# Off-diagonal products of the delta net's triangular inverse, queued behind one more projection tile

## The chip, the cores and the metric

The kernel runs on one core of a Trainium2 chip. The metric is the device time of one execution in microseconds (us). The core has a matrix engine (TensorE, PE in the profile, with its weight loads as PEld), a vector engine (VectorE, DVE), a scalar engine (ScalarE, ACT), a general engine (GpSimd, POOL), and SyncE (SP), which here issues nearly all DMAs. Each engine works through one queue of instructions in order. A matmul writes into PSUM, and another engine has to read the result out ("evict" it) before that buffer can be written again.

## The reference

Two layers of a diffusion trunk run on 1152 tokens (1024 latent and 128 context tokens) of width 1024. Each layer is a token mixer and an MLP, each between modulated norms:

```
x = x + gate1 * norm(mixer(modulate(norm(x))))
x = x + gate2 * norm(w2 . relu(w1 . modulate(norm(x)))^2)
```

The mixer has one input projection that feeds four groups of heads: latent attention, windowed attention, a gated delta net that runs over the tokens in both directions, and a Hyena long convolution. Their outputs go through one output projection. The delta net is computed in chunks of 64 tokens:

```
a   = tril(kb . k^T * gam, -1)                    # 64 x 64 per chunk and head
sol = triangular_solve(a + I, [v*b, kb*exp(decay)])
u_v, w = sol[..., :dv], sol[..., dv:]
def step(S, xs):                                   # one chunk after the other
    u = uv_c - w_c . S
    o = qd_c . S + aqk_c . u
    return S * tl_c + kt_c^T . u, o
```

The triangular solve is what the change touches: the kernel builds the inverse of (a + I), transposed, for every chunk, head and direction, and multiplies with it.

## The kernel before

All large products are taken in three reduced-precision products (high x high, high x low, low x high), so a tile of projections is 3 chunks of tokens (384 columns each) x 8 slices of the width x 3 products = 72 matmuls. `proj_tile` (L499) makes one such tile of 128 output columns: each chunk gets a PSUM buffer `pj` from a pool of four (`self.P`, pool "P", L313), and its `sink` evicts it. For the Hyena tiles the sink (L518, L519) is two reads of `pj` by ACT. The token-major transposes of a Hyena tile (`ht`, three of them, evicted by ACT at L1748) take their buffers from the same four.

In each layer three Python generators are advanced by turns (`run_timed`), each by a clock of its own: `rest` makes the projections and then Hyena and attention, `other` prepares the delta net and scans it, and `adas` makes the modulation vectors of later stages (`ada`, with its weights `wada` by DMA). Whatever `other` emits is given a higher priority, and the scheduler of the framework then settles the order of each engine's queue by these priorities and by its own reckoning of times. The Hyena stage (`X`, `iz`) and the attention (`S`, `ST`, `O`) follow the projections in `rest`.

The tiles of a layer come in a fixed order: delta net inputs (5 tiles), its gate (2), six Hyena tiles (8th to 13th), the windowed values (14th), the latent keys (15th), two tiles of queries (16th, 17th), and four rotary tiles (18th to 21st).

`gdn_prep` runs once for each pair of heads, p = 0 and then p = 1. Around the change it does this:

- 31 steps of forward substitution on diagonal blocks of 32 (`N`, L1205 to L1214); direction 0 on DVE, direction 1 on POOL.
- ACT writes a transposed copy `Tb` of each `N` (L1217), SP writes `N` and `Tb` to DRAM (`nscr`, L1218, L1219) and reads them back in another layout: `NT` (L1229) and `NaT`, which lies in the tile `NaTG` (L1232).
- The off-diagonal blocks `G` are two small products one after the other: st = 0 is AT x NaT (32 x 32 each, 72 for two heads' worth of chunks), evicted by DVE (L1251), and st = 1 multiplies with NT and is evicted by ACT (L1257).
- Then `kd`, `wt` and `uv` follow with NT, and after p = 1 the scan `gdn_scan`: 18 serial steps, each with products `u` and `dS` on PE that wait for one another through DVE and ACT. Its outputs go to DRAM (`goscr<-sc`), from where the normed output is read (`o`).

The keys of the latent attention (`mla_keys`: `ct`, `kpT`, `k`, `v`) are also made in the stretch in which p = 1 is prepared.

Of the kernel before, what the change touches and what calls it, by code (L numbers as in the profile page):

```python
# [29 lines left out]
AT = 2  # L30
# [133 lines left out]
class Trunk:  # L164
# [334 lines left out]
    def proj_tile(self, l, j, hi, lo, sink, w=None):  # L499
        w = w or self.load_cols(self.I["wa"][l, j], "wa")  # L500
        for a, n in NCH:
            ps = self.P(name="pj")
            for k in range(8):
                self.mm3(ps[:, :n], w(k), [hi[k][:, a:a + n], lo[k][:, a:a + n]], k == 0, k == 7)
            sink(ps[:, :n], slice(a, a + n))

    def proj_raw(self, l, j, hi, lo, name):
        o = self.W(name=name)
        self.proj_tile(l, j, hi, lo, lambda ps, s: self.nc.scalar.copy(out=o[:, s], in_=ps))
        return o  # L510
# [579 lines left out]
    def gdn_prep(self, l, p, g, be, tag):  # L1090
# [76 lines left out]
        AQ, AT = [], []  # L1167
# [53 lines left out]
        NaT, G = X[:, 0], X[:, 1].rearrange("p m h c -> p h m c")  # L1221
# [12 lines left out]
            NTm.append(NT)  # L1234
        yield

        for st in range(2):
            for h in range(2):
                pg = self.P((9, 32), "G", "Q")
                for m in range(9):  # L1240
                    for dr in range(2):
                        ab, bb = dr * 32, 32 - dr * 32
                        for a in range(2):
                            ra = slice(a * 64 + ab, a * 64 + ab + 32)
                            rb = slice(a * 64 + bb, a * 64 + bb + 32)
                            if st == 0:
                                self.mm(pg[rb, m], AT[dr][ra, m, h, bb:bb + 32], NaT[ra, m, h])
                            else:
                                self.mm(pg[ra, m], G[rb, h, m], NTm[dr][rb, m, h, bb:bb + 32])
                if st == 0:  # L1250
                    V.tensor_copy(out=G[:, h], in_=pg[:, :9])  # L1251
                else:
                    for dr in range(2):
                        for a in range(2):
                            ra = slice(a * 64 + dr * 32, a * 64 + dr * 32 + 32)
                            bb = 32 - dr * 32
                            nc.scalar.activation(out=NTm[dr][ra, :, h, bb:bb + 32], in_=pg[ra, :9], func=AF.Copy, scale=-1.0)  # L1257
            yield
# [765 lines left out]
    def sink(self, l):  # L2024
        def f(kt, ps, s):
            w = s.stop - s.start
            t = self.H(name="osk")
            self.nc.scalar.copy(out=t[:, :w], in_=ps)
            self.nc.sync.dma_start(out=self.oscr[l, kt, :, s], in_=t[:, :w])
        return f  # L2030
# [5 lines left out]
    def layer(self, l):  # L2036
# [54 lines left out]
        if l == 0:  # L2091
            with self.tc.issue_after(self.lead.ins):
                self.late_consts()
        self.done = set()

        def until(x):
            while x not in self.done:
                yield 1
# [142 lines left out]
```

## Time and profile before

| | |
|---|---|
| median of 3 runs | 3825.18 us (3819.07 to 3829.11) |
| profiled execution, its own time | 3828.84 us |
| its span, first to last instruction | 3827.1 us |
| mean granted clock of TensorE | 0.938 of full speed |
| PE busy | 3531.1 us (92%) |
| DVE, ACT, POOL busy | 2279.6, 1355.6, 853.1 us |

The stages of a layer follow one another. In layer 0 the projections with the preparation of the delta net lie between about 150 and 490 us, the scan with Hyena between 490 and 680 us, the attention after that up to about 1010 us, and the MLP up to about 1900 us, in which PE is never idle. In layer 1 the same stages lie at about 2000 to 2375, 2375 to 2606, 2606 to 3000 and 3050 to 3811 us.

In a row of the timeline stand start, duration, engine, line, operation, output and inputs, partitions x elements, how many instructions were merged, and in brackets the idle time of the engine before it with what ended it.

### The profile page before, as it was taken

The numbers are of one execution on the slowest core, as the hardware profiler recorded it, in microseconds if no ns is written. First come the engines' busy times: TensorE is split into PE (matmuls) and PEld (weight loads), VectorE is DVE, ScalarE is ACT, GpSimd is POOL, SyncE is SP. The second block draws the span as 40 slices with busy tenths as digits, with TensorE's granted clock in tenths as the row PEclk, the third lists the DMA queues.
The fourth block names the chain that finished last, engine by engine and source line by source line (L and its number), as shares of the span: only waits on it lengthen the run. The fifth ranks groups of instructions, "written<-read, shape, count | busy, mean of one in ns | idle before, by whom it ended". The sixth has DMA issues, their size and how long they took to land. (4 is left out here: it accounts for less than half of the span.)

```text
span 3827.1 us, 57478 instructions
## 1 busy us (share of the span) xinstructions
PE 3531.1 (92%) x21710; PEld 2958.8 (77%) x21710; DVE 2279.6 (60%) x4583; ACT 1355.6 (35%) x2970; POOL 853.1 (22%) x806
## 2 busy tenths in 40 slices
PE   7989888899899999999989798787999999999998
PEld 4879764366689999999968797645666899999997
DVE  5765577696645444444586664768884544444446
ACT  5434343264542222122354234323564422222112
POOL 1151521264430000000131524213553200000003
PEclk9999889897899999999999898897889999999999
DMA  5356486831421111111234465756314211111113
GB/s 202 115 120 158 139 275 202 235 90 39 138 87 47 45 44 34 44 45 45 96 103 131 108 144 161 258 187 177 84 50 138 72 45 45 45 45 42 40 41 121
DMA packets 364672, 405.31 MB, mean 106 GB/s; under 512 B 115815, under 2 KB 237157, under 8 KB 364394
## 3 DMA queue, kind: packets, MB, share of 16 engines
q1 hardware_dynamic: 364394, 401.63, 34.9%
q8 instruction: 171, 2.80, 0.3%
q14 instruction: 107, 0.88, 0.1%
HBM read 298.34 MB, written 103.19 MB: 105 GB/s over the span
## 5 line engine op out<-in xcount | busy, mean ns | idle before, releaser
L213 PE MATMUL hid<-hT,w1h 128*128 128x384 f32 x3072 | 786.5, 335 | 0.1
L213 PE MATMUL pj<-hT,wah 128*128 128x384 f32 x2112 | 575.1, 351 | 9.0 <-ACT wah L253 4.2
L1831 DVE TENSOR_TENSOR acc<-acc,mo 128x512 f32<-128x512 f32 x504 | 346.1, 687 | 391.8 <-PE mo L213 391.8
L213 PEld LDWEIGHTS hid<-hT,w1h 128*128 128x128 f32 x3072 | 557.7, 188 | 14.4 <-ACT h L481 1.1
L213 PE MATMUL hid<-hT,w1l 128*128 128x384 f32 x1536 | 514.1, 335 | 0.0
L213 PE MATMUL mo<-w2h,ul 128*128 128x512 f32 x1116 | 435.0, 392 | 0.0
L213 PE MATMUL mo<-w2h,uh 128*128 128x512 f32 x1080 | 422.7, 391 | 0.0
L213 PE MATMUL mo<-w2l,uh 128*128 128x512 f32 x1080 | 422.7, 391 | 0.0
L213 PEld LDWEIGHTS pj<-hT,wah 128*128 128x128 f32 x2112 | 395.3, 196 | 21.9 <-issue 7.8
L662 POOL TENSOR_TENSOR e<-e,e 128x512 f32<-128x512 f32 (+1 forms) x216 | 307.3, 1424 | 313.8 <-DVE el L232 145.2
L269 POOL TENSOR_TENSOR postr<-postr,mhalf 128x1 f32<-128x1 f32 x36 | 22.3, 621 | 1568.9 <-DVE postr L268 1568.6
L213 PE MATMUL pj<-hT,wal 128*128 128x384 f32 x1056 | 367.5, 348 | 0.7 <-DVE wal L232 0.7
L242 ACT CAST w2h<-w 128x512 fp32r<-128x512 f32 x128 | 70.3, 619 | 732.9 <-PE mo L213 728.8
L213 PEld LDWEIGHTS hid<-hT,w1l 128*128 128x128 f32 x1536 | 288.3, 188 | 2.5
L232 DVE TENSOR_TENSOR el<-e,eh 128x512 fp32r<-128x512 f32 (+1 forms) x252 | 241.4, 977 | 25.1 <-ACT eh L653 20.4
L213 PEld LDWEIGHTS mo<-w2h,ul 128*128 128x128 f32 x1116 | 209.6, 188 | 46.1
L213 PEld LDWEIGHTS mo<-w2h,uh 128*128 128x128 f32 x1080 | 202.8, 188 | 37.5
L213 PEld LDWEIGHTS mo<-w2l,uh 128*128 128x128 f32 x1080 | 202.7, 188 | 36.5
L213 PEld LDWEIGHTS pj<-hT,wal 128*128 128x128 f32 x1056 | 206.3, 195 | 4.6 <-issue 2.0
L1814 DVE SCALAR_TENSOR_TENSOR relu<-hid,relu 128x384 f32<-128x384 f32 x180 | 99.5, 554 | 166.9 <-ACT relu L1813 166.9
L213 PE MATMUL ada<-wada,cst 128*32 128x512 f32 x384 | 130.8, 692 | 45.5 <-DMA wada<-in_w_ada 45.4
L232 DVE TENSOR_TENSOR wal<-wa,wah 128x512 fp32r<-128x512 f32 x88 | 67.6, 773 | 147.2 <-ACT wah L253 118.2
(502 smaller groups left out, 6366.6 us busy)
## 6 DMA issues: line engine op xcount, KB each, us to landing
w<-in_w SPq DMA_DIRECT2D x256, 256.0 KB
wada<-in_w_ada SPq DMA_DIRECT2D x192, 256.0 KB
wa<-in_wa SPq DMA_DIRECT2D x88, 256.0 KB
x<-xres SPq DMA_DIRECT2D x21, 512.0 KB
x<-in_x SPq DMA_DIRECT2D x18, 512.0 KB
Q<-rscr SPq DMA_DIRECT2D x32, 288.0 KB
o<-oscr SPq DMA_DIRECT2D x18, 512.0 KB
xres<-x SPq DMA_DIRECT2D x36, 256.0 KB
```

The source lines that it names most:

```text
L213: self.last = self.nc.tensor.matmul(out, l, r, start=start, stop=stop, skip_group_check=True)
L232: self.nc.vector.tensor_tensor(out=lo, in0=x, in1=hi.bitcast(F32), op=ALU.subtract)
L242: self.nc.scalar.copy(out=hi[:, q], in_=st)
L269: self.nc.gpsimd.tensor_tensor(out=out, in0=out, in1=self.bcs(self.mhalf[:out.shape[0]], out.shape), op=ALU.pow)
L662: self.nc.gpsimd.tensor_tensor(out=acc, in0=acc, in1=e, op=ALU.add)
L1814: nc.vector.scalar_tensor_tensor(out=r[:, :n], in0=ps[:, :n], scalar=0.0, in1=r[:, :n], op0=ALU.max, op1=ALU.mult)
L1831: nc.vector.tensor_tensor(out=acc[t][:, ns], in0=acc[t][:, ns], in1=ps, op=ALU.add)
```

## The change

Each tile of projections now leaves its last matmul in a list (`tiles`, emptied for each layer). In `gdn_prep`, ahead of the off-diagonal products, the generator waits until 11 (p = 0) or 18 (p = 1) tiles have been emitted, handing the turn to the other generators meanwhile. The products of st = 0 then get an order edge: on PE they stand behind the last matmul of the newest tile. Nothing is computed differently, and no instruction is added.

```diff
@@ proj_tile
             sink(ps[:, :n], slice(a, a + n))
+        self.tiles.append(self.last)
@@ gdn_prep
+        while len(self.tiles) < (11, 18)[p]:
+            yield 3
+        behind = self.tiles[-1]
         for st in range(2):
             for h in range(2):
                 pg = self.P((9, 32), "G", "Q")
...
                             if st == 0:
-                                self.mm(pg[rb, m], AT[dr][ra, m, h, bb:bb + 32], NaT[ra, m, h])
+                                with self.tc.issue_after(behind.ins):
+                                    self.mm(pg[rb, m], AT[dr][ra, m, h, bb:bb + 32], NaT[ra, m, h])
@@ layer
         self.done = set()
+        self.tiles = []
```

Three places in the queues are shown, since the edge and the later emission together move instructions over a wide stretch. The numbers in the names are serial numbers of buffers and differ between the two kernels. The first place is PE's queue in layer 0, p = 0, before the change: the end of the 10th tile, its transposes, and what follows.

```order
L213 MATMUL pj_2839<-hT_417,wal_2783 128x384
L229 MATMUL ht_490_3013<-ident,hc_2523 128x128 x4
L229 MATMUL ht_492_3021<-ident,hc_2523 128x128 x4
L229 MATMUL ht_494_3029<-ident,hc_2523 128x128
L213 MATMUL G_2446<-NaTG_2429,Q_1876 32x32
L213 MATMUL G_2484<-NaTG_2429,Q_1876 32x32
L213 MATMUL G_2446<-NaTG_2429,Q_1876 32x32
L213 MATMUL G_2484<-NaTG_2429,Q_1876 32x32
L213 MATMUL pj_3048<-hT_403,wah_3038 128x384
```

The same place now:

```order
L213 MATMUL pj_2634<-hT_417,wal_2578 128x384
L229 MATMUL ht_464_2665<-ident,hc_2447 128x128 x4
L229 MATMUL ht_466_2673<-ident,hc_2447 128x128 x4
L229 MATMUL ht_468_2681<-ident,hc_2447 128x128
L213 MATMUL pj_2700<-hT_403,wah_2690 128x384
```

The first four G products stood ahead of the 11th tile (`pj_3048`); now the 11th tile (`pj_2700` and its two further chunks) follows the transposes at once, and all of G stands behind it. The second place is ACT's queue at the same time, as it was before (`pj_2839` is the third chunk of the 10th tile):

```order
L518 COPY hcx_2771<-pj_2812 128x384
L519 ACTIVATE hc_2772<-pj_2812,hcw_1400 128x384
L253 CAST wah_3329<-wa_3327 128x512
L1217 COPY Tb_2425<-N_2014 72x1024
L253 CAST wah_3335<-wa_3333 128x512
L518 COPY hcx_2771<-pj_2839 128x384
L519 ACTIVATE hc_2772<-pj_2839,hcw_1400 128x384
L1748 COPY hu_3018<-ht_490_3013 128x512
```

And now (`pj_2634` is the third chunk of the 10th tile):

```order
L519 COPY hcx_2566<-pj_2607 128x384
L520 ACTIVATE hc_2567<-pj_2607,hcw_1400 128x384
L253 CAST wah_3015<-wa_3013 128x512
L1218 COPY Tb_2425<-N_2014 72x1024
L253 CAST wah_3021<-wa_3019 128x512
L519 COPY hcx_2566<-pj_2634 128x384
L520 ACTIVATE hc_2567<-pj_2634,hcw_1400 128x384
L1753 COPY hu_2670<-ht_464_2665 128x512
```

Nothing moved there: in both kernels the copy `Tb` of direction 1 stands ahead of the two reads of the 10th tile's third chunk. The third place is PE's queue at the end of the scan in layer 1, before the change (`u` and `dS` are the scan's, `S` the attention's first products, `ada_24190` the last of eight such products that follow the scan's last `u`):

```order
L213 MATMUL ada_24190<-wada_24565,cst 32x512
L229 MATMUL oT_24174<-ident,o_24143 128x128 x4
L229 MATMUL oT_24180<-ident,o_24143 128x128 x4
L229 MATMUL oT_24186<-ident,o_24143 128x128
L229 MATMUL adat_24570<-ident,adarow_24568 128x128 x4
L213 MATMUL S_24583<-K_24485,Q_24483 128x384
```

And now (the last `ada` products stand a few rows ahead of these):

```order
L213 MATMUL dS_24029<-u_24024,sc_23768 64x64 x2
L213 MATMUL dS_24029<-u_24024,kt_22409 64x64 x2
L229 MATMUL adat_24570<-ident,adarow_24568 128x128 x4
L213 MATMUL S_24583<-K_24389,Q_24387 128x384
L213 MATMUL S_24586<-K_24389,Q_24387 128x384
L213 MATMUL S_24589<-K_24389,Q_24387 128x384
L213 MATMUL S_24589<-Q_24387 128x128
L213 MATMUL dS_24035<-u_24024,sc_23768 64x64 x2
L213 MATMUL dS_24035<-u_24024,kt_22411 64x64 x2
L213 MATMUL u_24084<-St_3975_22415,sc_23950 64x64
```

Before, all 18 steps of the scan stood ahead of the first `S`; now 16 do in layer 1 (17 in layer 0), and the rest stand among the attention's products. The last `ada` products stood behind the whole scan, and now stand ahead of its last two steps. In layer 1, 216 matmuls of projections stood behind the scan's first product, and 113 do now (234 and 208 in layer 0).

## Rows read from the trace of the kernel before

**Rows 1.** The page: busy time of PE, and its clock in 40 slices.
```profile
PE 3531.1 (92%) x21710; PEld 2958.8 (77%) x21710; DVE 2279.6 (60%) x4583; ACT 1355.6 (35%) x2970; POOL 853.1 (22%) x806
...
PEclk9999889897899999999999898897889999999999
```

**Rows 2.** Waits of PE: what waited, for what, us in total, times, longest.
```profile
PE ada L213 <- DMA wada<-in_w_ada: 45.4, 24, 14.5
PE G L213 <- DMA NaTG<-nscr: 30.7, 5, 18.3
```

**Rows 3.** Timeline of PE, layer 0, p = 0.
```profile
284.18 0.79 PE L213 MATMUL G<-NaTG,Q 32*32 32x32 f32 x8 [18.32 <-DMA NaTG<-nscr]
284.90 1.01 PE L213 MATMUL pj<-hT,wah 128*128 128x384 f32 x2
...
290.64 0.51 PE L213 MATMUL pj<-hT,wah 128*128 128x384 f32 x2
...
291.17 0.52 PE L213 MATMUL pj<-hT,wah 128*128 128x384 f32 x2
```

**Rows 4.** Timeline of ACT at the same time.
```profile
280.71 1.96 ACT L1217 COPY Tb<-N 72x1024 f32<-72x1024 f32 x1 [15.39 <-POOL N L1212]
...
283.08 0.48 ACT L518 COPY hcx<-pj 128x384 f32<-128x384 f32 x1
283.45 0.59 ACT L519 ACTIVATE hc<-pj,hcw 128x384 f32<-128x384 f32 x1
```

**Rows 5.** Timeline of PE, layer 1, p = 0.
```profile
2175.34 0.41 PE L213 MATMUL G<-NaTG,Q 32*32 32x32 f32 x4 [8.57 <-DMA NaTG<-nscr]
...
2180.49 0.39 PE L213 MATMUL G<-NaTG,Q 32*32 32x32 f32 x4 [2.51 <-DMA NaTG<-nscr]
2180.81 1.01 PE L213 MATMUL pj<-hT,wah 128*128 128x384 f32 x2
```

**Rows 6.** Timeline of ACT at the same time.
```profile
2171.52 1.96 ACT L1217 COPY Tb<-N 72x1024 f32<-72x1024 f32 x1 [1.35 <-POOL N L1212]
...
2175.61 0.60 ACT L519 ACTIVATE hc<-pj,hcw 128x384 f32<-128x384 f32 x1
```

**Rows 7.** Stretches: us, busy us of each engine (instructions), PE's clock, DMA share, GB/s.
```profile
281.20:301.70 20.50, 15.68 (x338) 14.20 (x338) 9.66 (x7) 6.53 (x13) 9.16 (x5) 0.75 0.57 129
...
2179.00:2196.00 17.00, 12.70 (x316) 11.46 (x317) 5.34 (x6) 4.17 (x10) 3.76 (x2) 0.70 0.33 85
```

**Rows 8.** Timeline of PE, layer 0, p = 1: the keys.
```profile
423.51 1.11 PE L229 MATMUL ct<-ident,ckv 128*128 128x128 f32 x4 [3.31 <-POOL ckv L553]
...
432.40 2.93 PE L213 MATMUL k<-cT,ukv 128*128 128x512 f32 x6 [4.91 <-ACT cT L525]
```

**Rows 9.** Timeline of PE, layer 1, p = 1: two transposes before the keys.
```profile
2309.52 0.47 PE L229 MATMUL tt<-ident,ckvT 128*128 128x128 f32 x1 [5.69 <-DVE mn L526]
2313.84 0.47 PE L229 MATMUL svt<-ident,svT 128*128 128x128 f32 x1 [3.85 <-ACT ckv L1086]
```

**Rows 10.** The scan's first products, layer 0 then 1: duration ns, first and last start.
```profile
L213 PE MATMUL u<-St,sc x144: 218/267/366, 489.1 to 670.8; 64*64 64x64 f32 x144
...
L213 PE MATMUL u<-St,sc x144: 218/267/366, 2373.2 to 2570.2; 64*64 64x64 f32 x144
```

**Rows 11.** Stretches of PE on the tile u alone: us, busy (instructions), clock, DMA.
```profile
550.00:600.00 50.00, 7.76 (x288) 0.97 0.72 247
```

**Rows 12.** Timeline of PE, layer 1, from the scan's end to the attention.
```profile
2575.41 0.45 PE L213 MATMUL u<-u,Q 64*64 64x64 f32 x8
2590.41 4.00 PE L213 MATMUL ada<-wada,cst 128*32 128x512 f32 x8 [14.54 <-DMA wada<-in_w_ada]
2600.96 3.87 PE L213 MATMUL ada<-wada,cst 128*32 128x512 f32 x8 [6.56 <-DMA wada<-in_w_ada]
...
2606.16 0.77 PE L213 MATMUL S<-K,Q 96*128 96x384 f32 x3
```

**Rows 13.** Timeline of SP's queue in that stretch.
```profile
2577.84 0.34 SPq L1384 DMA_DIRECT2D goscr<-sc  x1
```

## The prediction

> **What bounds the kernel now.** I read the page first. PE is busy for 92% of the span [rows 1], so little of the 3827.1 us is PE's idle time, and a change that moves PE's work gains only where PE stands still or runs at its lower clock (1.2 instead of 2.4 GHz). The clock dips in the slices of the projections, the scan and the attention, not in the MLP [rows 1]. The list of PE's waits comes next: the products G wait for the transfer of NaT 5 times, 30.7 us in all [rows 2]. That is 0.8% of the time and what the change can take away directly. The timeline then shows where: 18.32 us in layer 0 [rows 3], 8.57 and 2.51 us in layer 1 [rows 5], all at p = 0; the two others share the remaining 1.3 us, in layer 1 at p = 1.
>
> A stall of an in-order queue is only worth its length if the next work in the queue could have run. So for each of these stalls I looked for what the next tile of projections waits for.
>
> **Layer 0, p = 0.** The order shows that nothing but the four first G products stands between the transposes of the 10th tile and the 11th tile. The 11th tile needs a PSUM buffer from the pool of four. The last four taken are the third chunk of the 10th tile and its three transposes, so the next one is the buffer of that third chunk. It comes free when ACT has read it twice (L518, L519). These two reads stand on ACT behind the copy Tb of direction 1, which waits 15.39 us for the last POOL step of the substitution [rows 4]. The reads run from 283.08 and end at 283.45 + 0.59 = 284.04 [rows 4]. G starts at 284.18 [rows 3]. So two locks hold PE here and open within 0.14 us of each other. The change removes the first one only: ACT's queue is the same as before at this place, and so the 11th tile starts at about 284.1 rather than at 284.90 [rows 3]. Gain: 0.8 us, plus or minus a small wait among the later G products. I take **-1 us** (0 to -2).
>
> A page of the Trainium skill, "Perfetto Trace Analysis" (section "Optimization Strategy"), says that a gap on the engine that should be saturated can mean that there isn't enough SBUF or PSUM for the next tile to be allocated. Here that rule speaks against the change: by it the pool of four buffers keeps the gap, and this term is -1 us; by the list of waits alone, which names only the transfer, it would be -18.3 us. Which of the two holds is the first thing that the trace of after will show.
>
> **Layer 1, p = 0.** The same two locks, but here they don't open together. PE waits 8.57 us before the first G products, and 2.51 us before the last ones, and the 11th tile starts at 2180.81 [rows 5]. On ACT the copy Tb of direction 1 starts at 2171.52 and the last read of the 10th tile ends at 2175.61 + 0.60 = 2176.21 [rows 6]. So the 11th tile can start at 2176.2 instead of 2180.81: 4.6 us. I take **-5 us** (-4 to -7).
>
> **The lower clock.** In the 20.5 us from 281.2 the mean clock is 0.75, and in the 17 us from 2179 it is 0.70 [rows 7]. Two projection matmuls of wah take 1.01 us in the first and 0.51 us a little later [rows 3]. At most a quarter of 20.5 us and 0.30 of 17 us, 5 us each, are lost by this. PE still stands idle for some 18 us in layer 0 and for some 10 us in layer 1 before the 11th tile, so I take nothing back: **0** (0 to -10).
>
> **p = 1 and the keys.** In layer 1 two transposes wait 5.69 and 3.85 us [rows 9] behind the substitution on DVE and the copy Tb on ACT; with p = 1 emitted later, Tb stands behind the copies of the keys there, and these 9.5 us and the 1.3 us of G go. But in layer 0, where the substitution lies on top of the keys already, the keys wait 3.31 and 4.91 us on PE, and with smaller gaps between them more [rows 8]; the order of after gives layer 1 the same picture. So 10.8 us go and 8.2 us or a few more come: I take **0** (-8 to +8). In layer 0 the picture stays, with both ends some microseconds later: **0** (-5 to +5).
>
> **The scan and what follows.** This is the part that the diff doesn't show. The whole preparation of p = 1 is later, and in layer 1 some 103 more matmuls of projections (216 less 113) stand ahead of the scan. At the full pace, three matmuls in the 0.53 us from 290.64 to 291.17 [rows 3], these are 18 us. The scan is a serial chain: its first products start between 2373.2 and 2570.2 in layer 1 [rows 10], which is 197 us for 17 steps, 11.6 us a step; in layer 0 181.7 us, 10.7 us a step. Fewer steps lie beside projections, and the rest moves to the end, where it now lies beside the attention.
>
> What is at the end? In layer 1 PE finishes the scan's last products at 2575.9, waits 14.54 us and then 6.56 us for weights of ada, and starts the attention at 2606.16 [rows 12]. The transfers of these weights stand on SP behind the last scan outputs, at 2577.84 [rows 13]. In the order of after the last ada products and their transfers stand ahead of the scan's last two steps, and the attention's first products come two steps earlier than the scan's end. So the scan's first product is 12 to 18 us later, but the attention waits only for 16 steps of it: 2 x 11.6 = 23 us less, and for no ada behind the scan: up to 21 us less. I don't expect all of it, since the weights keep their limited buffers and DVE has as much to do as before; of 14.54 + 6.56 = 21.1 us I take **-15 us** (0 to -25). In layer 0 the attention follows the scan directly and the move is by one step: **-3 us** (-10 to +10).
>
> The price: the scan's work itself now runs beside the attention. On PE it is 7.76 us for 288 instructions [rows 11], and a step has 64 of them, so 1.7 us a step; with some waits of in-order queues (the scan's evictions behind the attention's on DVE and ACT) I take 2 us for each of 2.5 steps in layer 1 and 1.5 in layer 0: **+8 us** (+4 to +46, where the upper end is four steps of 11.6 us laid bare).
>
> **Sum.** -1 - 5 + 0 + 0 - 15 - 3 + 8 = -16 us. The sum is made against the profiled execution (3828.84 us), and gives 3812.8 us. That execution is 3.7 us above the median of the runs, so against the median the forecast is 3825.2 - 16 = **3809 us**, 0.4% less.
>
> **Rivals.**
>
> *The stalls go entirely.* If the 11th tile isn't held by ACT (because the scheduler's order is one thing and the buffers another, or because ACT isn't late any more), the 30.7 us [rows 2] and both halves of the clock's loss (10 us) come back: 3825 - 41 = 3784 us. For it speaks that the trace names only the transfer as the wait; against it the 0.14 us between the two locks. By the Trainium skill, "TensorE: Matmul & The Clock Gate" (section "HAM oscillation"), it would have to be both or neither, since an idle wait for a transfer makes the next work start at the lower clock; the dip from 281.2 us behind the 18.32 us agrees.
>
> *The stall only moves.* G's wait becomes a wait of the projections in both layers, and the later stages come out even: -1 - 5 = -6, so 3819 us, within the noise. For it speaks that the terms of the later stages are the least certain of the sum.
>
> *The scan is laid bare (slower).* The scan is the only serial chain here, and the change starts it later. If the attention's products, in order on PE, DVE and ACT, wait for the steps among them, the 2.5 + 1.5 steps cost up to 11.6 us each instead of 2, and the gain at the end is not made: -6 + 46 = +40, so 3865 us at most, and 3842 at half of it (-6 + 23). It decides from 4.4 us of bare time a step (4 x 4.4 = 6 + 11.5). For it speaks that PE already waits for DVE inside the scan, and that the attention has less of PE idle to give; against it that the attention of before doesn't start until 30 us after the scan in layer 1. I price it at 3850 us.
>
> **How the numbers follow.** A difference under 0.3% (11.5 us) can't be told from no change here. The forecast has 0.50, with an own spread of about 3797 to 3820: 0.34 of it is faster by over 0.3% and 0.16 within. The stalls that go entirely have 0.14 (faster), the moved stall 0.16 (within), the bare scan 0.20 (slower). Together: faster 0.48, within 0.32, slower 0.20. The range reaches down to 3780, which takes in the first rival, and up to 3842, the bare scan at half its price; outside lie a bare scan at its full price and a sum of all the lower ends.
>
> **What would show it.** Right: in layer 0 the wait of some 18 us before 284 is still there, now before a `pj`, released by ACT; in layer 1 the 11th tile starts some 4 to 6 us earlier; the `ada` waits at the scan's end in layer 1 shrink and `S` starts well before 2600. Wrong: a PE without a gap before the 11th tile in layer 0 (the first rival), or u and dS with long waits beside the attention, and the attention's end later than 3000 us (the third). New keys' waits in layer 1 above 15 us would break the zero that I took there.

## The result: slower, and the profile after

The changed kernel takes 3851.27 us in the median of 5 runs (3842.78 to 3868.85), the kernel before 3824.66 us. The ratio is 1.0072, with a 95% interval of 1.0053 to 1.0091: slower by 0.7%, clear of noise. A second set of its runs (experiment e11) gave 1.0057 (1.0041 to 1.0074). The forecast was 3809 us, and the range ended at 3842: wrong, and to the other side.

The profiled execution took 3842.78 us with a span of 3841.0 us, 13.9 us more than the span before. The medians are 26.6 us apart. So the trace shows about half of the loss; where the rest lies in the longer runs, no trace shows.

PE's busy time is the same. The page, as [rows 1] for before:

```profile
PE 3531.7 (92%) x21710; PEld 2951.8 (77%) x21710; DVE 2286.6 (60%) x4583; ACT 1361.5 (35%) x2972; POOL 864.0 (22%) x806
...
PEclk9999888896999999999999898996989999999999
```

3531.7 us against 3531.1: nearly all of the 13.9 us is time in which PE stands idle. The list of PE's waits after (what waited, for what, us in total, times, longest), as [rows 2]:

```profile
PE ada L213 <- DMA wada<-in_w_ada: 30.5, 21, 6.0
PE pj L213 <- ACT hc L520: 18.3, 3, 16.4
PE ct L229 <- POOL ckv L554: 14.9, 2, 9.7
PE ST L213 <- DMA Q<-mscr: 11.4, 1, 11.4
```

The 30.7 us in which G waited for NaT [rows 2] are down to 0.9 us, and 15 us of the waits for `ada` weights are gone. In their place stand a wait of the projections for ACT, waits of the keys (`ct`), and one of the attention's main products (`ST`). The first of them is the stall of layer 0, in the timeline of PE, as [rows 3]:

```profile
281.84 1.01 PE L213 MATMUL pj<-hT,wah 128*128 128x384 f32 x2 [16.44 <-ACT hc L520]
```

and ACT at that time, as [rows 4]:

```profile
278.45 1.96 ACT L1218 COPY Tb<-N 72x1024 f32<-72x1024 f32 x1 [12.93 <-POOL N L1213]
280.31 0.62 ACT L253 CAST wah<-wa 128x512 fp32r<-128x512 f32 x1
280.82 0.48 ACT L519 COPY hcx<-pj 128x384 f32<-128x384 f32 x1
281.19 0.59 ACT L520 ACTIVATE hc<-pj,hcw 128x384 f32<-128x384 f32 x1
```

The stall is still there, two microseconds shorter, before a `pj`, and released by ACT's second read at 281.19 + 0.59 = 281.78. The scan starts later, as [rows 10] (first and last start):

```profile
L213 PE MATMUL u<-St,sc x144: 218/267/367, 2398.8 to 2600.0; 64*64 64x64 f32 x144
```

That is 25.6 us later than in [rows 10], in an execution whose layer 0 had ended its MLP's last products 5.6 us later.

The time of some first instructions shows where the loss is made. Each number is a first start in the profiled execution (us); the last column of a layer is the difference.

| | layer 0 before | after | diff. | layer 1 before | after | diff. |
|---|---|---|---|---|---|---|
| scan, first u | 489.1 | 496.0 | +6.9 | 2373.2 | 2398.8 | +25.6 |
| attention, first S | 681.9 | 679.6 | -2.3 | 2606.2 | 2586.9 | -19.3 |
| scan, last u<-St,qT | 671.5 | 691.1 | +19.6 | 2570.5 | 2600.7 | +30.2 |
| first ST | 724.2 | 731.3 | +7.1 | 2636.4 | 2625.1 | -11.3 |
| first O | 729.4 | 736.4 | +7.0 | 2643.0 | 2648.8 | +5.8 |
| output projection | 1012.1 | 1021.3 | +9.2 | 2894.3 | 2907.4 | +13.1 |
| MLP | 1124.1 | 1131.3 | +7.2 | 3011.6 | 3024.6 | +13.0 |

Up to the first S the changed kernel is ahead, by 2.3 us in layer 0 and by 25 us in layer 1 (19.3, and the 5.6 us that it started late). From the first S to the first O it loses 9.3 and 25.1 us. In layer 1 that uses up the lead, and the 7.4 us that are lost by its MLP (13.0, less the 5.6) come behind the first O. Single executions are a weak measure of such differences: those of e9 and e10 (below), whose order in layer 0 is that of before, start the MLP of layer 0 9.7 us later and 1.5 us earlier than the kernel before. From the first S to the first O is the stretch in which the scan's last steps stand among the products S. The timeline of DVE in layer 1 shows how they meet (`mx` is the row maximum of S at L768; `St`, `u`, `sc`, `Q` are the scan's):

```profile
2592.64 2.07 DVE L768 TENSOR_REDUCE mx<-S 128x1 f32<-128x384 f32 x4
2594.74 0.23 DVE L1367 TENSOR_TENSOR u<-u,sc 128x64 f32<-128x64 f32 x1
...
2595.37 2.08 DVE L768 TENSOR_REDUCE mx<-S 128x1 f32<-128x384 f32 x4
2597.73 0.21 DVE L1386 TENSOR_TENSOR sc<-sc,u 64x64 f32<-64x64 f32 x1 [0.28 <-ACT sc L1385]
...
2611.68 0.17 DVE L735 TENSOR_SCALAR nm<-esy 128x8 fp32r<-128x8 f32 x1
```

and PE at the end of it:

```profile
2608.62 0.69 PE L213 MATMUL S<-K,Q 96*128 96x384 f32 x1 [1.73 <-DVE mx L768]
...
2613.36 0.42 PE L229 MATMUL mT<-ident,nm 128*8 128x128 f32 x1
2625.13 1.19 PE L213 MATMUL ST<-Q,K 97*128 97x512 f32 x2 [11.35 <-DMA Q<-mscr]
```

The 24 row maxima of the first head are ready at 2611.7, 24.8 us after the first S; then they go through DRAM into a row of Q, and ST waits 11.35 us for that with nothing else in PE's queue. Before, 33 row maxima were done in 22.4 us (2606.2 to 2628.6), other S products stood between, and the same wait was 2.4 us.

So the row maxima explain little of the 25.1 us. They are ready 2.4 us later behind the first S than before, and ST starts 8.0 us later behind it (38.2 instead of 30.2 us); most of that is their way through DRAM, 9.9 us from ACT's copy (`mrow`) to ST instead of 4.7. The other 17.1 us lie between the first ST and the first O (23.6 instead of 6.5 us). Here stand, on PE, the transposes `oT` of the delta net's normed output, which follow the end of the scan by way of DRAM, POOL and DVE. Before, they were done ahead of most of the S products:

```profile
2604.76 1.20 PE L229 MATMUL oT<-ident,o 128*128 128x128 f32 x9
...
2613.30 2.18 PE L229 MATMUL oT<-ident,Q 128*128 128x128 f32 x9 [0.58 <-DVE Q L1422]
...
2642.98 0.40 PE L213 MATMUL O<-eh,VA 128*128 128x512 f32 x1
```

and after, ahead of the first O:

```profile
2639.32 2.12 PE L229 MATMUL oT<-ident,o 128*128 128x128 f32 x9
...
2645.81 2.12 PE L229 MATMUL oT<-ident,Q 128*128 128x128 f32 x9
...
2648.77 0.40 PE L213 MATMUL O<-eh,VA 128*128 128x512 f32 x1
```

The first O is not quite the same point of the work in both, since 45 ST products stand between the first ST and the first O after and 15 before: a part of the 17.1 us is order and not loss. In layer 0, where the transposes stand ahead of the first ST in both kernels, the row maxima are ready 4.3 us later behind the first S, and ST starts 9.4 us later behind it.

The attention as a whole, from the first S to the output projection (us, busy us of PE, PEld, DVE, ACT, POOL, PE's clock, DMA share, GB/s), before, layer 0 and 1:

```profile
681.90:1012.10 330.20, 293.42 (x1258) 187.38 (x1257) 243.74 (x424) 163.20 (x328) 157.42 (x109) 0.85 0.41 109
...
2606.20:2894.30 288.10, 261.39 (x1178) 184.60 (x1177) 240.23 (x388) 160.82 (x324) 153.53 (x108) 0.85 0.33 86
```

and after:

```profile
679.60:1021.30 341.70, 301.40 (x1354) 191.93 (x1353) 256.39 (x452) 170.97 (x355) 157.81 (x110) 0.84 0.40 107
...
2586.90:2907.40 320.50, 277.59 (x1323) 194.09 (x1321) 255.40 (x454) 172.05 (x357) 161.58 (x110) 0.81 0.33 88
```

In layer 1 the attention takes 32.4 us more: PE is idle for 42.9 instead of 26.7 us, and busy for 16.2 us more, with 145 more matmuls in the stretch (136 of them the scan's) and a clock of 0.81 instead of 0.85.

### The profile page after: what moved, and what is told of

Same layout as the page of the kernel before. It is cut to its first block, busy times and chain, and to the rows that moved or that the text cites. A ratio compares the mean times of both kernels' runs of the same rounds, so it can differ in the third digit from the quotient of the medians.

```text
span 3841.0 us, 57437 instructions
## 1 busy us (share of the span) xinstructions
PE 3531.7 (92%) x21710; PEld 2951.8 (77%) x21710; DVE 2286.6 (60%) x4583; ACT 1361.5 (35%) x2972; POOL 864.0 (22%) x806
```

## Experiments

The theory formed from the two traces is **late scan**: the change makes the scan start later, its last steps come to stand among the attention's first products, and there they cost more than all that the projections gain. Its rival at first was **late keys**: p = 1 is prepared on top of the keys in layer 1 too. All ratios are to runs of the kernel before on the same chip.

**e1 and e2: one part alone.** The edit of e1 (that of e2 is the same for p = 1 and 18 tiles):

```diff
-        while len(self.tiles) < (11, 18)[p]:
+        while p == 0 and len(self.tiles) < 11:
             yield 3
...
-    with self.tc.issue_after(behind.ins):
+    with self.tc.issue_after(behind.ins) if p == 0 else contextlib.nullcontext():
```

> The change at p = 0 alone (wait for 11 tiles, order edge); p = 1 as before. In the order the scan then starts as late as in the changed kernel (113 projection matmuls behind its first product in layer 1, and 1 and 2 steps left at the first S). Theory 'late scan' (the loss is made where the scan's last steps stand among the attention's S products): as slow as the changed kernel, about 3850 us, 15 to 35 us over the kernel before. Rival 'late keys' (the loss comes from p = 1 being prepared on top of the keys): most of the loss is gone, 3818 to 3830 us.

> The change at p = 1 alone (wait for 18 tiles, order edge); p = 0 as before. In the order 144 projection matmuls stand behind the scan's first product in layer 1 (216 before, 113 in the changed kernel), and half a step is left at the first S. 'Late scan': between the two, 3826 to 3840 us. 'Late keys': as slow as the changed kernel, about 3850 us.

Measured: e1 1.0079 (1.0055 to 1.0103), e2 1.0019 (0.9998 to 1.0039). The part at p = 0 makes the whole loss, the part at p = 1 little or none. That speaks for late scan: in e1 the order at the scan is that of the changed kernel, although p = 1 has neither wait nor edge; it is only late because p = 0 is.

**e3: the wait without the order edge.**

```diff
-    with self.tc.issue_after(behind.ins):
+    with contextlib.nullcontext():
```

> The generator still waits for 11 and 18 tiles, but without the order edge on PE. In layer 0 the order is that of before again at the scan, in layer 1 it lies between (150 projection matmuls behind the scan's first product, no step left at the first S). 'Late scan': 3820 to 3832 us. If it is the late emission itself that costs: about 3850 us.

Measured: 1.0079 (1.005 to 1.0108), a miss for late scan. No step of the scan stands among the S products there, and the kernel is as slow. In its one trace G waits 37.9 us for NaT (two stalls of 19 us), and layer 0 alone loses 22 us by its MLP, spread over the preparation (5), the scan with Hyena (11) and the attention (6). So late scan can't be the whole account: emitting the delta net later costs time in more ways than one, and which one this is, isn't settled.

**e4: S behind the scan.** The changed kernel, with an order edge that restores one feature of the order of before:

```diff
             scan(0, i)
             if i < 2:
                 scan(16, i)
+            self.scanned = self.last
...
-    self.mm(ps[:, :384], q, K[0][:96, 384 * a:384 * a + 384])
+    with self.tc.issue_after(self.scanned.ins) if h == 0 else contextlib.nullcontext():
+        self.mm(ps[:, :384], q, K[0][:96, 384 * a:384 * a + 384])
```

> The changed kernel, with one more order edge: the S products of the first attention head stand behind the scan's last product on PE, as they did before the change. 'Late scan' in its narrow form (the loss is the mixing of the scan's last steps with S): S starts later, about 690 and 2606 us, but the stretch from S to ST takes 42 and 30 us as before, and the time falls to 3825 to 3840 us. If the late end of the scan costs by itself, mixed or not: 3845 to 3870 us.

Measured: 3831.8 us, 1.0015 (0.9999 to 1.0032), as expected by late scan in its narrow form. S starts at 688.6 and 2581.6, and ST comes 37.4 and 27.5 us behind it (51.7 and 38.2 in the changed kernel, 42.3 and 30.2 before). That S would wait until 2606 in layer 1 was a miss: it starts 24 us earlier. DVE after the scan's last step in layer 1:

```profile
2588.82 7.71 DVE L769 TENSOR_REDUCE mx<-S 128x1 f32<-128x384 f32 x15
...
2600.08 0.16 DVE L735 TENSOR_SCALAR nm<-esy 128x8 fp32r<-128x8 f32 x1
```

Fifteen row maxima run through in 7.7 us, and the row maxima of the head are ready 18.5 us after the first S. Undoing the mixing gives back 0.4 to 0.6% (1.0072 and 1.0057 against 1.0015). But it doesn't beat the kernel before: its attention in layer 1 still takes 308.2 us (288.1 before).

```profile
2581.60:2889.80 308.20, 276.73 (x1186) 191.41 (x1184) 245.07 (x419) 164.19 (x331) 154.63 (x110) 0.80 0.32 84
```

The 20 us more lie behind the first O. Up to there it takes 37.0 us (36.8 before); from there to the output projection, before and in e4:

```profile
2643.00:2894.30 251.30, 230.86 (x1076) 161.35 (x1075) 209.89 (x327) 153.12 (x310) 150.82 (x107) 0.87 0.27 66
...
2618.60:2889.80 271.20, 248.13 (x1091) 169.94 (x1089) 214.82 (x345) 151.61 (x305) 143.90 (x105) 0.82 0.26 64
```

PE is busy for 17.3 us more there, with nearly as many matmuls and at a lower clock, and idle for 2.6 us more. So in its trace e4 leads the changed kernel by 13.8 us at the MLP of layer 0, where one step had mixed, and by only 3.5 us more at that of layer 1, where two had.

**e5, e6, e7: the double lock.** The copies Tb leave ACT, in the changed kernel (e5), in e4 (e6), and in the kernel before (e7):

```diff
-    nc.scalar.copy(out=Tb[:72], in_=N[dr][:72].rearrange("p r c -> p c r"))
+    (V, nc.gpsimd)[dr].tensor_copy(out=Tb[:72], in_=N[dr][:72].rearrange("p r c -> p c r"))
```

> The changed kernel, with the copies Tb taken off ACT: direction 0 on DVE, direction 1 on POOL, each behind its own substitution. Theory 'double lock' (the 11th tile at p = 0 waits for ACT's reads of the 10th tile's third chunk, which stand behind Tb): the wait of the 11th tile for ACT (16.4 us in layer 0 of the changed kernel) is gone, the tile starts at about 265 us instead of 282, and what is left is a wait of G of at most 6 us behind it. 12 us a layer come free in the projections; what the scan and the attention leave of them: 3815 to 3850 us. Rival (the tile waits for something else, its weights or DVE): the wait stays, with another releaser.

> Both repairs: Tb off ACT, and the S products of the first attention head behind the scan's last product. If both causes hold and add up, it beats the kernel before: 3800 to 3822 us. If the time freed in the projections is lost again later whatever the order, 3825 to 3845 us.

> The kernel before, with Tb off ACT and nothing else. G still stands ahead of the 11th tile, so the 18 us wait for NaT in layer 0 stays (double lock: both have to go): 3820 to 3832 us, unless the scheduler moves the scan, where 'late scan' expects more.

Measured: e5 1.0092 (1.0064 to 1.012), e6 1.0074 (1.0046 to 1.0102), e7 1.0047 (1.0027 to 1.0066). The lock is shown, the gain isn't. PE in layer 0 of e5:

```profile
265.42 0.62 PE L213 MATMUL pj<-hT,wah 128*128 128x384 f32 x2 [0.41 <-ACT hc L520]
...
286.09 0.28 PE L213 MATMUL G<-NaTG,Q 32*32 32x32 f32 x2 [7.91 <-DMA NaTG<-nscr]
287.16 0.31 PE L213 MATMUL G<-NaTG,Q 32*32 32x32 f32 x2 [0.79 <-DMA NaTG<-nscr]
294.62 0.31 PE L213 MATMUL G<-NaTG,Q 32*32 32x32 f32 x2 [7.14 <-DMA NaTG<-nscr]
296.10 2.04 PE L213 MATMUL G<-NaTG,Q 32*32 32x32 f32 x136 [1.18 <-DMA NaTG<-nscr]
```

With Tb off ACT the 11th tile starts at 265.4, 16.4 us earlier than in the changed kernel. Then G, behind it, waits 17 us for NaT all the same. And the keys (`ct`) start at 420.9, 2.8 us later than in the changed kernel, the scan at 502.0, 6 us later. The preparation is a chain through the substitution, DRAM and G, and filling PE beside it didn't shorten it. But the chain itself was later here: POOL starts the last step of the substitution at 282.24 instead of 278.15, and SP issues the last load of NaT at 293.73 instead of 286.26. So what the 16.4 us would be worth with the chain at its old times, e5 doesn't show. e6 against e4 (1.0074 against 1.0015) is slower as well, with the same copies moved; what they cost besides isn't settled. The expectation of a kernel faster than before failed. In e7 the scheduler moved the scan as well (144 projection matmuls behind its first product in layer 1 instead of 216), so it isn't a clean control for Tb; the wait for NaT stayed, at 22 us in layer 0 and 26.8 us in layer 1.

**e8: p = 1 alone, with S behind the scan.** The edits of e2 and e4 together.

> The change at p = 1 alone, plus the order edge that keeps the first head's S products behind the scan's last product. The half step that mixed with S in each layer no longer does. If mixing costs in proportion to the steps, 5 us a layer come back from the p = 1 kernel (1.0019): 3820 to 3832 us, about the kernel before; if 'late scan' costs even without mixing, 3832 to 3845 us.

Measured: 3844.28 us, 1.0039 (1.0014 to 1.0063): in the range for a late scan that costs even without mixing. The edge brings nothing where only half a step mixes (e2: 1.0019, the intervals overlap), and the kernel is not better than before. Nor is its gain clear with Tb off ACT, where whole steps had mixed (e5 1.0092, e6 1.0074, the intervals overlap). It is clear from the changed kernel to e4, and from e9 to e10 below.

**e9 and e10: only the scan is late.** The kernel before, in which nothing but the scan is held back (e10 adds the edge of e4):

```diff
         load(8)
         load(0)
+        while len(self.tiles) < (18, 20)[l]:
+            yield 3
+        behind = self.tiles[-1]
         for i in range(16):
...
-    self.mm(pu[h][ra, p, k], w, St[half(h), dr, p], k == 0 and p == 0, k == 1)
+    with self.tc.issue_after(behind.ins) if s == 0 else contextlib.nullcontext():
+        self.mm(pu[h][ra, p, k], w, St[half(h), dr, p], k == 0 and p == 0, k == 1)
```

> The kernel before, in which only the scan is held back: its first product stands on PE behind the 20th tile of layer 1 (72 projection matmuls behind it instead of 216); layer 0 is in the order of before, and so are G and both preparations. In layer 1 two steps of the scan stand among the S products, as in the changed kernel. 'Late scan' with mixing: layer 1 loses 10 to 25 us, 3836 to 3852 us. If the loss of the changed kernel needs the moved preparation: within 8 us of the kernel before.

> The same held-back scan, with the S products of the first head behind the scan's last product. If mixing is what a late scan costs: 10 us or more less than without the edge, 3824 to 3838 us. If the late end of the scan costs by itself: as slow as without it, or slower.

Measured: e9 3871.14 us, 1.0101 (1.0062 to 1.0141); e10 3845.37 us, 1.0055 (1.0035 to 1.0075). This is the cleanest pair: G and both preparations stand as before, and the late scan alone makes a loss as large as that of the change, or larger. Both are slower than expected. About half of the loss goes when the mixing is undone (25.8 us between the medians; the runs of the two overlap by one). The stretch from the first S to the first O in layer 1 of e9:

```profile
2602.00:2669.00 67.00, 44.50 (x279) 33.70 (x277) 44.67 (x118) 25.30 (x63) 14.12 (x8) 0.59 0.55 161
```

and of e10:

```profile
2601.20:2635.40 34.20, 29.28 (x106) 22.49 (x106) 30.59 (x76) 12.67 (x26) 10.79 (x6) 0.57 0.75 223
```

67.0 us with two steps among the products, 34.2 without, 36.8 before. PE is idle for 22.5 us of it in e9 and for 4.9 us in e10. The mixing puts 45 instead of 27 ST products ahead of the first O here as well, so the price of it is better read from the whole attention: from the first S to the output projection 332.2 us in e9 and 303.5 us in e10 (288.1 before). The other half of the loss stays in e10, and it lies behind the first O: from there to the output projection e10 takes 269.3 us in layer 1, the kernel before 251.3. Of these 18 us more, 12 are busy time of PE, as in e4 at a lower clock than before (0.84 instead of 0.87):

```profile
2635.40:2904.70 269.30, 242.79 (x1088) 167.03 (x1087) 214.29 (x346) 151.93 (x306) 145.69 (x105) 0.84 0.26 64
```

**e11: the changed kernel again.**

> The changed kernel once more, for a second profiled execution. If the first profile was typical, its stretches return within 3 us: about 52 and 38 us from the first S to the first ST, 7 and 6 us lost in layers 0 and 1. Its runs lie between 3842 and 3869 us again.

Measured: 50.0 and 37.2 us from the first S to the first ST, as before; 2.6 us lost in layer 0 and 9.1 in layer 1 (7.2 and 5.8 in the first trace), so the split between the layers moves by some 4 us from one execution to the next, their sum hardly. Its runs lie between 3841.51 and 3860.16.

**e12: an earlier scan.** If late is bad, is earlier good? The kernel before, with

```diff
-    run_timed((rest(), 1.5), (ahead(other()), GD), (adas(), 1))
+    run_timed((rest(), 1.5), (ahead(other()), 4 if l == 0 else GD), (adas(), 1))
```

> The kernel before, with the generator of the delta net given its turn more often in layer 0 (a step counts 4 instead of 6): in the order the scan of layer 0 starts earlier (298 projection matmuls behind its first product instead of 234, and most of the keys behind it too); layer 1 is nearly as before (196 instead of 216). If a late scan costs because the scan ends a serial chain, an earlier one gains in layer 0: its MLP starts 5 to 15 us earlier, 3810 to 3822 us. If the scan of before was early enough (something else bounds the attention then): within 5 us in layer 0, 3820 to 3832 us.

Measured: 1.0114 (1.0092 to 1.0137), a clear miss. The scan of layer 0 starts only 3 us earlier, and what was moved back for it, the keys, starts 18.7 us later and Hyena 20.2 us. The loss of late scan is no rule that earlier is better: the delta net shares DVE, ACT and POOL with the keys and Hyena, and the order of before lies between two that lose.

## Why the prediction was wrong

**Layer 0, p = 0** (-1 us): right. The wait became one of the projections, released by ACT, as the double lock had it; e5 shows the other side, that the tile starts at once when the second lock is gone. It came out at -3.1 us, since POOL was done 2.3 us earlier. The rival in which the stalls go entirely fell with it. By the Trainium skill ("Perfetto Trace Analysis", section "Optimization Strategy") the same gap repeating on the engine that should be saturated can mean that there isn't enough PSUM for the next tile; the gap here comes once a layer, and in layer 0 the trace agrees with that cause, with 16.44 us before the tile that needed the buffer.

**Layer 1, p = 0** (-5 us): the mechanism was right, the size too large. The 11th tile starts at 2183.31 instead of 2180.81; less the 5.6 us by which the layer began late, 3.1 us are gained, and 1.7 us in the second trace.

**p = 1 and the keys** (0): too favourable in layer 1. The two transposes' waits went, but the keys wait longer than those of layer 0 from which the term was taken:

```profile
2319.27 1.11 PE L229 MATMUL ct<-ident,ckv 128*128 128x128 f32 x4 [9.71 <-POOL ckv L554]
2324.75 1.19 PE L213 MATMUL k<-cT,ukv 128*128 128x512 f32 x2 [3.52 <-DVE mn L527]
2329.83 2.07 PE L213 MATMUL k<-cT,ukv 128*128 128x512 f32 x4 [3.89 <-DVE cT L527]
2336.44 0.62 PE L213 MATMUL v<-ukv,cT 128*128 128x256 f32 x3 [2.23 <-DVE kk L527]
```

19.4 us, above the 15 us that the prediction named as its limit, and 8.6 us more than the 10.8 us that went: just beyond the upper end of the term, +8 us. In layer 0 the scan starts 6.9 us later, also beyond the 5 us given there.

**The clock** (0): it did come back a little in the preparation (0.89 to 0.92 in layer 0 from 200 us to the scan, 0.86 to 0.90 in layer 1), and was lost again in the attention.

**The scan and what follows** is the step that failed, in both of its terms. That the scan's first product would come later in layer 1 was right (20 us, less the 5.6; the prediction had 12 to 18). That the first S would come much earlier was right too (25 us), and so was that the `ada` waits at the scan's end would shrink (14.54 and 6.56 us to 6.0 and less). But I booked 15 us of this as gain, and in the changed kernel it all went again before the first O. And the price of the mixed steps, 2 us each on PE by its busy time (+8), was taken from the wrong engine. What the steps delay is two chains through other engines. One is the row maxima on DVE, behind which ST waits by way of DRAM. The other is the scan's own output, through DRAM, POOL and DVE to the transposes `oT`, which then stand on PE among the attention's first products. From the first S to the first O these cost 9.3 us in layer 0 and 25.1 us in layer 1, of which 17.1 us, part of it mere order, lie behind the first ST.

The gap of before, 30 us ahead of S in layer 1, was not empty: DVE was busy for 21.4 us of it, mostly with Hyena and the norm of the delta net's output. That this work then slows the attention is not shown. In layer 1, e4 and e10 leave under 1 us between the scan's last `dS` and the first S, with next to no mixing, and from the first S to the first O they lose nothing. Behind it they take 20 and 18 us more than before, but so do e12 and e7 (20 and 24 us), which keep 18 to 19 us of the gap and mix nothing there.

So of the rivals the third, the bare scan, came nearest: a slower kernel, with the gain at the end not made. That its price, 3850 us, is the measured time is luck. The 34.4 us of both layers from the first S to the first O would be 8.6 us for each of four steps, above the 4.4 us of its condition; but only 17.4 us of them, 4.4 us a step, lie ahead of the first ST, and the trace holds only half of the medians' difference. I gave it 0.20 because the attention of before began 30 us after the scan in layer 1, and read those 30 us as room.

What stays open: the half of the medians' difference that the traces don't hold, the loss of e3, and why PE runs at a lower clock behind the first O in e4 and e10 (0.82 and 0.84 instead of 0.87), where most of their 20 and 18 us are. The kernel before has one trace, and its 251.3 us there are the shortest of all traces.

## What to carry to other kernels

A stall of the busiest engine is worth its length only if the next work in its queue could run, and only if the stretch isn't paced by a chain beside it: ask for the second lock (here a PSUM buffer behind a copy on ACT), and then whether anything later waits for PE's progress there (the 11th tile of layer 0 came 3.1 us earlier, and the scan 6.9 us later). An order edge that delays the head of a serial chain should be priced where the chain ends: look at which work its last steps will then share queues with, and take the price from the chains that they hold up there, the way of their own output among them, not from their busy time. A gap in front of a stage isn't a gain by its length: look at what other engines do in it, and follow the change to the end of the stage, since a lead at its start was lost behind its first products here.

## What the runs showed of the hardware

TensorE was granted its lower clock (1.2 of 2.4 GHz) for tens of microseconds in which it was busy almost without a pause. In layer 1 of the kernel before (stretches of 5 us, columns as above) it fell behind a stretch in which PE had been busy for 2.98 of 5 us, waiting for DVE:

```profile
2735.00:2740.00 5.00, 5.00 (x23) 3.62 (x21) 5.00 (x9) 4.95 (x10) 3.03 (x3) 1.00 0.01 2
2740.00:2745.00 5.00, 2.98 (x11) 1.52 (x10) 5.00 (x7) 1.84 (x4) 4.76 (x4) 0.96 0.00 0
2745.00:2750.00 5.00, 5.00 (x15) 3.45 (x16) 4.39 (x12) 0.00 (x0) 1.78 (x2) 0.50 0.00 0
...
2765.00:2770.00 5.00, 5.00 (x14) 3.07 (x13) 2.50 (x6) 0.98 (x3) 3.63 (x3) 0.50 0.91 204
2770.00:2775.00 5.00, 5.00 (x31) 3.89 (x30) 3.53 (x6) 3.94 (x8) 1.40 (x2) 0.81 0.21 46
```

It rose again some 27 us later, though PE was never idle in between. In the changed kernel the longest such stretch of this layer's attention takes in 2800 to 2830 us, behind 3.49 busy us of 5; its first 10 us have pauses of 0.37 and 0.47 us:

```profile
2795.00:2800.00 5.00, 3.49 (x9) 1.50 (x9) 5.00 (x7) 1.07 (x2) 4.10 (x3) 0.83 0.00 0
2800.00:2805.00 5.00, 4.63 (x14) 3.13 (x14) 3.07 (x12) 0.00 (x0) 0.00 (x0) 0.50 0.00 0
...
2825.00:2830.00 5.00, 5.00 (x14) 3.29 (x14) 2.60 (x8) 1.38 (x3) 1.27 (x1) 0.50 0.00 0
2830.00:2835.00 5.00, 5.00 (x31) 3.42 (x30) 2.68 (x7) 1.28 (x3) 0.73 (x1) 0.76 0.12 27
```

In the first of these stretches PE has 13 to 15 matmuls in most of the stretches at 0.50, and 23 in the one at 1.00 that stands ahead. So a stretch of 25 to 30 us at the lower clock costs an estimated 13 to 15 us, half of its length. That it fell because of the short waits ahead of it isn't shown. It may be part of why the runs of the changed kernels spread over 20 to 30 us; no run here tests it.
